# Sixty-four bytes of padding behind one constant: every tile on the left side of SBUF starts half a 128-byte line later

## The chip, the cores and the metric

The kernel runs on one core of one Trainium2 chip. The metric is device time in microseconds (us), the median of the runs shown; lower is better. The core has a matrix engine (PE, with its weight loads shown apart as PEld), a vector engine (DVE), a scalar engine (ACT), a general engine (POOL), a sequencer that mostly issues transfers (SP), and 16 DMA engines. On-chip memory (SBUF) has 128 partitions. A tile takes the same range of bytes in each partition, and "the byte a tile starts at" below is its offset inside a partition. Matrix products accumulate in a separate memory, PSUM.

## The reference

One layer of a streaming encoder on `x` (1, 512, 1024), all in float32:

```python
proj = x @ w_in                       # 1024 x 5704: queries, keys, values of two mixers, index, gates
y_a  = dsa_sequence(q_a, k_a, v_a, q_i, k_i, w_i, rel_bias)   # sparse attention: top-128 keys by an indexer, T5 bias
y_s  = sb_sequence(q_s, k_s, v_s)     # stick-breaking attention, strictly causal
merged = sigmoid(g_a + b0) * (y_a @ w_branch_dsa) + sigmoid(g_b + b1) * (y_s @ w_branch_sb)
x = layer_norm(2**0.25 * x + merged @ w_out)
u, g = split(x @ w_ffn_in)            # 1024 x 5632
h = gelu(causal_dwconv(u)) * g        # width 3, over 2816 channels
x = layer_norm(2**0.25 * x + h @ w_ffn_out)                   # 2816 x 1024
```

The constant of this case is `bgt`, the two gate biases `b0` and `b1`: 16 float32 numbers for each of 128 partitions.

## The kernel before, in words

Every float32 product is made of three matrix multiplications in the type float32r: each operand is split into a high part (ACT copies it to float32r) and a low part (DVE subtracts the high part), and high x high, high x low and low x high are added up in PSUM. A helper, `Stream`, brings the weights: SP issues 512 KB loads into three `raw` buffers, ACT makes `whi` (line 104) and DVE makes `wlo` (line 113), each in three ring buffers. The order of the pieces is one list, and the work of the two mixers is laid out by hand with projections as fillers between the attention heads, so that the matrix engine always has something to do. The scheduler is given ties (`issue_after`) where the order matters.

The stages are: indexer queries and first values (to about 25 us), index scores and key selection, eight stick-breaking heads, eight sparse heads (to about 320 us), the branch products, the output projection (`out_proj`, lines 866 to 868) with the first layer norm, the up-projection of the channel mixing (`ffn_in`, lines 937 to 939, from about 390 us), in which the first down-projection products (`product`, lines 1017 to 1019) are woven in, then the rest of the down-projection in a seven-product scheme, and the second layer norm (to the end at 744.9 us).

In a matrix multiplication one operand is held in the array (stationary, loaded by a PEld instruction) and the other streams through it (moving). In the projections (`proj_t`, lines 233 to 235) and in `ffn_in` the stationary operand is a weight from the ring and the moving one is the activation; in `proj_v` (lines 270 to 272), `out_proj` and `product` the weight is the moving operand.

SBUF is given out as two stacks. The left stack grows up from byte 0 and begins with 16,384 reserved bytes and four small constants; then come the pool `cst` (`ident`, `mhalf`, `bgt`, `cwt`, `wi`), the three `raw` buffers, the ring, and the pools of each stage. The right stack grows down from the top and begins with a pool `edge` that holds one tile of 32 bytes, `rb`; then come the activations `xh` and `xl`, the gate and branch tiles, and later `x1h`, `x1l`, the residual rows `r` and the layer norm's rows. Each allocation is rounded up to 32 bytes. A helper `padded` gives a small tile a whole number of 128-byte units, and nearly all small tiles are made with it:

```python
    def padded(pool, shape, dt=F32, **kw):

        n = int(np.prod(shape[1:]))
        t = pool.tile([shape[0], -(-n // 32) * 32], dt, **kw)[:, :n]
        return t if len(shape) == 2 else t.rearrange("p (a b) -> p a b", a=shape[1])
```

`mhalf` (4 bytes, rounded to 32), `bgt` (64) and `cwt` (352) are not. In the built program `ident` starts at byte 16,512, `mhalf` at 17,024, `bgt` at 17,056, `cwt` at 17,120, `wi` at 17,472, the first `raw` buffer at 17,600. From `wi` on, every tile of the left side starts at byte 64 modulo 128, and so does every tile of the right side (`rb` at 229,312, `x1h` at 170,688).

Of the kernel before, what the change touches and what calls it, by code (L numbers as in the profile page):

```python
# [11 lines left out]
F32 = mybir.dt.float32  # L12
# [115 lines left out]
def tile_block(ctx: ExitStack, tc: tile.TileContext, xT, xN, w_qi, w_ki, w_t, w_v, w_br, w_o, w_fi, w_fo,  # L128
# [10 lines left out]
# [6 lines that stand above are left out]
    cst = ctx.enter_context(tc.tile_pool(name="cst", bufs=1))  # L145
# [74 lines left out]
    nc.gpsimd.memset(mhalf, -0.5)  # L220
    nc.scalar.activation(mhalf, mhalf, AF.Sigmoid)
    nc.gpsimd.memset(mhalf, -0.5)
    bgt = cst.tile([128, 16], F32, name="bgt")
    cwt = cst.tile([128, FC, 4], F32, name="cwt")


# [1072 lines left out]
```

## Time and profile before

| | us |
|---|---|
| median of 3 runs (range) | 747.27 (746.85 to 747.35) |
| span of the profiled execution, first to last instruction | 744.9 |
| median less that span | 2.4 |
| PE busy in that span | 735.6 (99%) |
| PEld, DVE, ACT, POOL busy | 616.9, 572.0, 408.0, 148.8 |

The page shows one execution. PE is busy nearly all the time, the others are not; PEld runs beside PE. The durations of matrix multiplications on the page overlap, so their rate is read from the starts of instructions that follow each other.

### The profile page before, as it was taken

What the parts mean: (1) busy time and instruction counts of PE and PEld (TensorE: products, weight loads), DVE (VectorE), ACT (ScalarE), POOL (GpSimd) and SP (SyncE); (2) the same over time, 40 slices, a digit from 0 to 9 for tenths busy, and PEclk for the clock granted to TensorE, in tenths of its full rate; (3) what the DMA queues carried; (4) which work ended last, traced back from release to release, by engine and by line L of the source; (5) the groups of instructions that cost most, each with busy time, mean ns of one, the idle gap of its engine ahead of it and who ended that gap; (6) DMA issues with size and microseconds to landing.
All of it is one profiled execution on the core that took longest, in us unless ns stands there. A gap on an engine that the chain in (4) does not pass through costs nothing.

```text
span 744.9 us, 9755 instructions
## 1 busy us (share of the span) xinstructions
PE 735.6 (99%) x3477; PEld 616.9 (83%) x3477; DVE 572.0 (77%) x907; ACT 408.0 (55%) x572; POOL 148.8 (20%) x161
## 2 busy tenths in 40 slices
PE   9999999999999999999999999999999999999995
PEld 7888888888888888888889888888888888888885
DVE  5569888999679898668755866686767668668985
ACT  6466867797785587845473533443444344345430
POOL 0002224365743332000101111011101101110011
PEclk9999999999999999999999999999999999999999
DMA  7445887796476455527832544444443444448632
GB/s 266 157 128 188 207 172 173 158 214 163 116 181 154 135 126 136 131 85 247 289 57 86 170 141 142 141 143 143 141 166 114 161 136 149 144 140 268 202 130 84
DMA packets 73631, 117.03 MB, mean 157 GB/s; under 512 B 42536, under 2 KB 42792, under 8 KB 73584
## 3 DMA queue, kind: packets, MB, share of 16 engines
q1 hardware_dynamic: 66304, 93.98, 42.0%
q0 software_dynamic: 5744, 18.38, 9.9%
q10 hardware_dynamic: 1536, 4.06, 2.1%
q8 instruction: 27, 0.44, 0.3%
q14 instruction: 20, 0.16, 0.1%
HBM read 95.93 MB, written 9.98 MB: 142 GB/s over the span
## 4 chain that ended last, share of the span: by engine, by line
PE 89%; DVE 3%; POOL 2%; issue 2%; DMA 2%; ACT 2%; DVEq 0%; POOLq 0%; ACTq 0%
PE u_ps L937 5%; PE u_ps L939 5%; PE g_ps L937 5%; PE u_ps L938 5%; PE g_ps L939 5%; PE g_ps L938 5%; PE m L1019 2%; PE m L1017 2%; PE m L1018 2%; PE av_ps L511 2%; PE ga_ps L234 2%; PE ga_ps L233 2%; PE gb_ps L235 2%; PE gb_ps L234 2%; PE ga_ps L235 2%; PE gb_ps L233 2%
## 5 line engine op out<-in xcount | busy, mean ns | idle before, releaser
L104 ACT ACTIVATE whi<-raw 128x1024 fp32r<-128x1024 f32 (+1 forms) x124 | 123.8, 1001 | 143.1 <-PE g_ps L938 43.7
L113 DVE TENSOR_TENSOR wlo<-raw,whi 128x1024 fp32r<-128x1024 f32 (+1 forms) x105 | 123.9, 1181 | 36.3 <-ACT whi L104 35.6
L939 PE MATMUL u_ps<-x1h,wlo 128*128 128x512 f32 (+1 forms) x192 | 71.4, 372 | 0.0
L937 PE MATMUL u_ps<-x1h,whi 128*128 128x512 f32 (+1 forms) x192 | 71.3, 372 | 0.0
L938 PE MATMUL u_ps<-x1l,whi 128*128 128x512 f32 (+1 forms) x192 | 71.3, 371 | 0.0
L937 PE MATMUL g_ps<-x1h,whi 128*128 128x512 f32 (+1 forms) x184 | 69.9, 380 | 0.0
L938 PE MATMUL g_ps<-x1l,whi 128*128 128x512 f32 (+1 forms) x184 | 69.9, 380 | 0.0
L939 PE MATMUL g_ps<-x1h,wlo 128*128 128x512 f32 (+1 forms) x184 | 69.9, 380 | 0.0
L939 PEld LDWEIGHTS u_ps<-x1h,wlo 128*128 128x128 f32 x192 | 36.2, 188 | 6.3
L938 PEld LDWEIGHTS u_ps<-x1l,whi 128*128 128x128 f32 x192 | 36.2, 188 | 6.3
L937 PEld LDWEIGHTS u_ps<-x1h,whi 128*128 128x128 f32 x192 | 36.2, 188 | 6.2
L939 PEld LDWEIGHTS g_ps<-x1h,wlo 128*128 128x128 f32 x184 | 34.6, 188 | 6.6
L938 PEld LDWEIGHTS g_ps<-x1l,whi 128*128 128x128 f32 x184 | 34.6, 188 | 6.5
L937 PEld LDWEIGHTS g_ps<-x1h,whi 128*128 128x128 f32 x184 | 34.6, 188 | 6.5
L960 DVE TENSOR_TENSOR t<-raw 128x512 f32<-128x512 f32 x11 | 7.6, 693 | 40.1 <-DMA raw<-in_w_fo_dram 39.2
L569 POOL TENSOR_TENSOR bm<-win,score 128x256 f32<-128x256 f32 (+2 forms) x24 | 26.9, 1147 | 32.2 <-DMA pl<-bm 27.3
L985 ACT ACTIVATE c<-c,cwt 128x512 f32<-128x512 f32 x22 | 15.9, 725 | 27.5 <-DVE c L984 27.3
L979 POOL MEMSET u<- 128x2 f32 x22 | 2.1, 98 | 143.7 <-ACT whi L104 99.2
L993 DVE TENSOR_TENSOR hF<-g_ps,c 128x512 f32<-128x512 f32 x22 | 15.1, 687 | 19.7 <-PE g_ps L939 19.7
L835 POOL TENSOR_TENSOR rstd<-rstd,mhalf 128x1 f32<-128x1 f32 x8 | 7.7, 959 | 104.6 <-DVE rstd L834 104.6
L423 DVE MAX8 m<-score 128x8 f32<-128x256 f32 (+2 forms) x48 | 26.6, 556 | 0.9
L557 POOL TENSOR_TENSOR beta<-beta,keep 128x1280 f32<-128x1280 f32 x8 | 21.6, 2704 | 26.7 <-DVE keep L554 26.7
(576 smaller groups left out, 2088.3 us busy)
## 6 DMA issues: line engine op xcount, KB each, us to landing
raw<-in_w_fi_dram SPq DMA_DIRECT2D x44, 512.0 KB, 3.3
raw<-in_w_t_dram SPq DMA_DIRECT2D x32, 512.0 KB, 3.7
raw<-in_w_fo_dram SPq DMA_DIRECT2D x26, 512.0 KB, 4.2
wlo<-in_w_t_dram POOLq DMA_DIRECT2D x14, 512.0 KB, 5.8
raw<-in_w_br_dram SPq DMA_DIRECT2D x8, 512.0 KB, 4.0
raw<-in_w_o_dram SPq DMA_DIRECT2D x8, 512.0 KB, 4.1
raw<-in_w_v_dram SPq DMA_DIRECT2D x7, 512.0 KB, 4.6
raw_b<-in_w_fo_dram SPq DMA_DIRECT2D x6, 512.0 KB, 5.5
```

Of the source, the lines that this page charges most:

```text
L104: self.high = nc.scalar.activation(hi[:, :w], t[:, :w], AF.Copy).ins
L113: self.done[key] = eng.tensor_sub(lo[:, :w], t[:, :w], r32(hi[:, :w])).ins
L233: nc.tensor.matmul(ps[:M], wh[:, c], xh[k], start=(k == 0), stop=False)
L234: nc.tensor.matmul(ps[:M], wh[:, c], xl[k], start=False, stop=False)
L235: nc.tensor.matmul(ps[:M], wl[:, c], xh[k], start=False, stop=(k == KC - 1))
L423: nc.vector.max(m8, sc)
L557: nc.gpsimd.tensor_mul(beta, beta, keep[:, 1:ATT + 1])
L569: nc.gpsimd.tensor_add(bm[:, OFF[j]:OFF[j] + N], win[:, 512 - N:512], score[j])
L937: nc.tensor.matmul(ps[:, c], wh[:, kc], x1h[:, k, c], start=(k == 0), stop=False)
L938: nc.tensor.matmul(ps[:, c], wh[:, kc], x1l[:, k, c], start=False, stop=False)
L939: nc.tensor.matmul(ps[:, c], wl[:, kc], x1h[:, k, c], start=False, stop=(k == KC - 1))
L985: nc.scalar.activation(c, c, AF.Gelu_apprx_tanh, bias=cwt[:, f, 3:4])
```

## The change

`bgt` is made by `padded`: 128 bytes are set aside for it instead of 64, and its 16 numbers stay at the front.

```diff
@@ -220,7 +220,7 @@
     nc.gpsimd.memset(mhalf, -0.5)
     nc.scalar.activation(mhalf, mhalf, AF.Sigmoid)
     nc.gpsimd.memset(mhalf, -0.5)
-    bgt = cst.tile([128, 16], F32, name="bgt")
+    bgt = padded(cst, [128, 16], name="bgt")
     cwt = cst.tile([128, FC, 4], F32, name="cwt")
```

In the two built programs 986 tiles lie in SBUF. 873 of them, all on the left side behind `bgt`, start 64 bytes later: `cwt` at 17,184, `wi` at 17,536 and the first `raw` buffer at 17,664. They start at byte 0 modulo 128 now (`cwt` at 32 instead of 96). The other 113, among them all tiles of the right side, stay where they were. The instructions of each engine, their order, and the semaphores that each waits for are the same in both programs.

## The prediction

> **What bounds the kernel now.** I read the page's first two lines, then the busy time by stage, then the starts of single matrix multiplications.
>
> ```profile
> span 744.9 us, 9755 instructions
> PE 735.6 (99%) x3477; PEld 616.9 (83%) x3477; DVE 572.0 (77%) x907; ACT 408.0 (55%) x572; POOL 148.8 (20%) x161
> 0.00:325.00 325.00, 323.19 (x1556) 271.25 (x1557) 262.69 (x484) 228.43 (x360) 100.57 (x90) 1.00 0.64 162
> 325.00:737.00 412.00, 412.00 (x1922) 345.49 (x1921) 304.82 (x415) 179.54 (x213) 47.27 (x70) 1.00 0.47 154
> 737.00:745.00 8.00, 0.38 (x4) 0.17 (x2) 4.46 (x11) 0.00 (x0) 0.92 (x1) 0.76 0.36 131
> ```
>
> The last three lines are stretches of the span (stretch, length, then busy time and count of PE, PEld, DVE, ACT, POOL, the granted clock, DMA share, GB/s). PE is idle for 1.8 us in the two mixers (325 less 323.19), for nothing at all in the 412 us after them, and for 7.6 us in the tail, where the second layer norm's last rows are made and sent. So the time is a count of matrix multiplications times their spacing, plus about 9.4 us. What does not change that spacing can win at most the 1.8 us, or something of the tail.
>
> The spacing is read from rows of the time line (start, length, engine, line, operation):
>
> ```profile
> 499.63 0.39 PE L1017 MATMUL R<-whi,ah 128*128 128x512 f32 x1
> 499.86 0.39 PE L1018 MATMUL R<-wlo,ah 128*128 128x512 f32 x1
> 500.08 0.39 PE L1017 MATMUL R<-whi,ah 128*128 128x512 f32 x1
> 500.31 0.39 PE L1018 MATMUL R<-wlo,ah 128*128 128x512 f32 x1
> ...
> 501.44 0.39 PE L937 MATMUL g_ps<-x1h,whi 128*128 128x512 f32 x1
> 501.67 0.39 PE L938 MATMUL g_ps<-x1l,whi 128*128 128x512 f32 x1
> 501.90 0.39 PE L939 MATMUL g_ps<-x1h,wlo 128*128 128x512 f32 x1
> 502.12 0.39 PE L937 MATMUL g_ps<-x1h,whi 128*128 128x512 f32 x1
> 399.94 0.28 PE L937 MATMUL u_ps<-x1h,whi 128*128 128x256 f32 x1
> 400.06 0.28 PE L938 MATMUL u_ps<-x1l,whi 128*128 128x256 f32 x1
> 400.18 0.28 PE L939 MATMUL u_ps<-x1h,wlo 128*128 128x256 f32 x1
> 400.30 0.28 PE L937 MATMUL u_ps<-x1h,whi 128*128 128x256 f32 x1
> ```
>
> Three steps of 512 columns take 0.68 us, 226.7 ns each; three of 256 take 0.36 us, 120 ns each. A column therefore costs (226.7 - 120) / 256 = 0.417 ns, and each multiplication carries 226.7 - 512 x 0.417 = 13.3 ns beside its columns. The spacing is the same where both operands come from the left side (line 1017: ring weights stream through `ah`) and where the moving one comes from the right (line 937: `x1h`). Today all of these begin at byte 64 modulo 128, so no row compares residues directly.
>
> **The change part by part.** The change removes no instruction, adds none and moves none; in the built programs order and waits are equal, and no tile of one stage comes to lie on another one that it would newly have to wait for. What it does is 873 new start bytes. I cost them by who reads or writes them.
>
> *Matrix multiplications.* The built program has 3,417 in float32r. In 2,298 the moving operand is on the right and the stationary on the left; in 877 both are on the left; in 242 the moving one is on the left, the stationary on the right. So 1,119 moving operands go from 64 to 0, and 3,175 stationary ones. For the moving side the bound below zero is that the whole 13.3 ns is the price of starting in the middle of a 128-byte line: 1,119 x 13.3 ns = 14.9 us. Two kinds of rows speak to it:
>
> ```profile
> 25.46 0.33 PE L313 MATMUL qi_ps<-xl,whi 128*128 128x384 f32 x1
> 25.64 0.33 PE L312 MATMUL qi_ps<-xh,whi 128*128 128x384 f32 x1
> 271.58 0.34 PE L511 MATMUL av_ps<-ptl,va 128*128 128x384 f32 x1
> 271.75 0.22 PE L511 MATMUL av_ps<-pth,va 128*128 128x128 f32 x1
> ```
>
> Line 313 streams 384 columns in one piece and takes 0.18 us to the next start; line 511 streams three pieces of 128 columns, 1,536 bytes apart, and each piece begins at byte 64 modulo 128. It takes 0.17 us. If a start at byte 64 cost 13.3 ns, two more of them would show as 27 ns. They do not, so I take zero for the moving side and keep the 14.9 us for the range.
>
> The Trainium skill, "TensorE: Matmul & The Clock Gate", section "Back-to-back issue gap", gives N / 2.4 + 2.5 ns, 215.8 ns for 512 columns; the rows above have 226.7, and the rule says nothing of start bytes or of float32r. If the missing 10.9 ns were the start byte, the left-moving 1,119 would give back 12.2 us, and the kernel would take 735.1.
>
> For the stationary side the cover is the multiplication that runs meanwhile:
>
> ```profile
> L939 PEld LDWEIGHTS u_ps<-x1h,wlo 128*128 128x128 f32 x192 | 36.2, 188 | 6.3
> L1018 PEld LDWEIGHTS R<-wlo,ah 128*128 128x128 f32 x22 | 4.1, 188 | 0.9
> ```
>
> A load takes 188 ns inside a spacing of 226.7; a start byte would have to cost 38 ns a load before PE waited at 512 columns. Without that cover, each further ns would cost 3.2 us over 3,175 loads. I take zero.
>
> *DVE, ACT and POOL.* They are late nowhere after 325 us, where PE has no idle time, and their cost there is zero even if they slow a little. Whether they do:
>
> ```profile
> L983 DVE SCALAR_TENSOR_TENSOR c<-u,cwt,c x22: 743/750/1401, 406.8 to 670.1; 128x512 f32<-128x512 f32 x22
> L840 DVE SCALAR_TENSOR_TENSOR r<-r,rstd,ln x14: 745/748/752, 365.6 to 736.5; 128x512 f32<-128x512 f32 x14
> ```
>
> Line 983 (the convolution's middle tap) reads `u` from 4 bytes behind its start, and `c` from its own; line 840 reads two tiles that start alike. The medians are 750 and 748 ns. Two inputs that lie 4 bytes apart in their lines cost 2 ns, so I take zero for 64 bytes as well. The tail's vector instructions read and write `r`, the layer norm's rows and `parts2`, all on the right: unchanged.
>
> *Transfers.* Loads into `raw` began at byte 192 modulo 256 and begin at 0 now; `xr` and `raw_qi`, which the first products wait for, went from 64 to 128.
>
> ```profile
> raw<-in_w_fi_dram SPq DMA_DIRECT2D x44, 512.0 KB, 3.3
> raw<-in_w_v_dram SPq DMA_DIRECT2D x7, 512.0 KB, 4.6
> 0.74 2.79 DMA xr<-in_xT_dram
> ```
>
> Equal loads land 3.3 to 4.6 us after issue depending on what runs beside them, a spread of 1.3 us that PE does not feel after 325 us. Before that, the 1.8 us of idle time bounds any gain. I take -0.1 us, between zero and -1.8, near zero because the ring holds three pieces ahead.
>
> The Trainium skill, "DMA: Bandwidth & Descriptors", section "How a descriptor splits into AXI transactions", says that a descriptor not starting at a multiple of 256 bytes pays for the bytes below its start. By its counting, stated for reads, 4,096 bytes from 192 would take 134 beats and from 0 take 128, 4.5% less. An estimate from it is 0.15 us of a 3.3 us load, and hidden; it speaks for the change, and no row here shows it.
>
> **The sum.** The profiled execution: 744.9 + 0 (moving) + 0 (stationary) + 0 (DVE, ACT, POOL) - 0.1 (transfers) = 744.8. The median of the runs lies 2.4 us above that span (747.27 - 744.9), which the change does not touch: 747.2 us. What a measurement can tell from no change is about 0.2%, 1.5 us: 745.8 to 748.8 counts as the same.
>
> **The rivals.**
>
> *The start byte is part of the 13.3 ns* (faster). For it: the 13.3 ns are there and nothing in the trace explains them, and they are the same for all operands, as they would be if all pay alike. Against it: the three-piece row. In full it gives 747.3 - 14.9 = 732.4; half of it, 739.8. Only left-moving lines (270 to 272, 511, 866 to 868, 1017 to 1019) would speed up, lines 937 to 939 not.
>
> *The two read streams of PE want the same residue* (slower). PE reads the moving operand and the next stationary one at the same time. Today both start at byte 64; afterwards 2,298 + 242 = 2,540 multiplications have one on each side, with residues that differ. For it: PE does run slower in places with no wait shown:
>
> ```profile
> 8.15 0.40 PE L271 MATMUL vs_ps<-wlo,xh 128*128 128x512 f32 x1
> 8.39 0.39 PE L272 MATMUL vs_ps<-whi,xl 128*128 128x512 f32 x1
> ...
> 9.54 0.39 PE L271 MATMUL vs_ps<-wlo,xh 128*128 128x512 f32 x1
> 9.77 0.39 PE L272 MATMUL vs_ps<-whi,xl 128*128 128x512 f32 x1
> ```
>
> Seven steps in 1.62 us are 231.4 ns, 4.7 ns above the steady spacing. At that price 2,540 of them cost 11.9 us: 759.2. It decides from 0.6 ns each (1.5 us). Against it: these slow steps appear with equal residues, and loads and streams are not in step with each other, so a fixed distance between starts need not matter.
>
> *Aligned loads land sooner* (faster, or the same). At most the 1.8 us of idle time before 325 us: 745.5, and for most of its chance under what can be told.
>
> *An engine with tiles on both sides slows* (slower, or the same). 29 two-input DVE instructions and 35 ACT ones touch both sides, few of them in the tail; behind PE they cost nothing, and if each lost 50 ns with PE waiting, 64 x 50 ns = 3.2 us: 750.5.
>
> That the change does not do what it says is excluded by the start bytes of the built program.
>
> **How the numbers follow.** No effect 0.60; start byte in the 13.3 ns 0.14; unequal residues 0.17; sooner loads 0.05, of which 0.03 over 0.2%; two-sided engines 0.04. Faster is 0.14 + 0.03 = 0.17, slower 0.17 + 0.04 = 0.21, the same 0.62. The likeliest case's own range is 745.8 to 748.8. For 8 in 10 I take in the first third of the first rival, down to 742.5 (14.9 / 3 is 5.0 us), and the first half of the second, up to 753.5 (11.9 / 2 is 6.0 us); beyond these I leave 0.09 and 0.08.
>
> **What would show it.** If I am right, the stretch from 325 to 737 us still has PE busy throughout, lines 937 and 1017 step by 226.7 ns, and line 113 keeps its duration. A step of 213 to 220 ns on line 1017 but 226.7 on line 937 is the first rival. A longer step on line 937 alone, or PEld above 188 ns, is the second. Equal steps with a shorter idle time before 325 us is the third; a longer DVE or ACT duration is the fourth.

## The result: 757.75 us, 1.4% slower

| | before | after |
|---|---|---|
| median of the runs compared (range), us | 747.19 (746.85 to 747.35) | 757.75 (757.58 to 758.17) |
| ratio after / before (95% interval) | | 1.0139 (1.0125 to 1.0153) |
| span of the profiled execution, us | 744.9 | 756.0 |

The forecast was 747.2 us, the range 742.5 to 753.5. The change costs 10.6 us in the medians and 11.1 us in the spans. Of all runs in this document one, of the kernel left_plus_256 below, took 1,619 us, for a reason that no trace shows; its median does not hang on it.

The page of after (first two lines), then the busy time by stage with the columns of the prediction's first fence:

```profile
span 756.0 us, 9755 instructions
PE 747.2 (99%) x3477; PEld 616.8 (82%) x3477; DVE 571.3 (76%) x907; ACT 409.4 (54%) x572; POOL 149.3 (20%) x161
```

```profile
0.00:325.00 325.00, 323.81 (x1541) 269.40 (x1542) 261.24 (x482) 228.69 (x359) 101.02 (x90) 1.00 0.63 162
325.00:748.00 423.00, 423.00 (x1936) 347.17 (x1935) 305.42 (x415) 180.71 (x213) 47.34 (x70) 1.00 0.44 150
```

PE is still busy without a gap from 325 us to the tail, at the full granted clock (1.00), and it is busy 11.6 us longer (747.2 against 735.6) for the same 3,477 instructions. DVE, ACT, POOL and PEld are busy as long as before, within 1.4 us each. So no new wait has appeared: the spacing of the matrix multiplications has grown (the idle time of PE before 325 us even fell, from 1.8 to 1.2 us). Where, the first and last starts of two lines tell. The view of one line's instructions (count, shortest, median and longest duration in ns, first and last start in us), of before and then of after:

```profile
L866 PE MATMUL o_ps<-wo0h,mh x8: 389/389/389, 347.3 to 385.4; 128*128 128x512 f32 x8
L939 PE MATMUL u_ps<-x1h,wlo x192: 278/389/389, 391.0 to 667.1; 128*128 128x512 f32 x160, 128*128 128x256 f32 x32
L939 PE MATMUL g_ps<-x1h,wlo x184: 283/389/389, 393.9 to 673.9; 128*128 128x512 f32 x168, 128*128 128x256 f32 x16
```

```profile
L866 PE MATMUL o_ps<-wo0h,mh x8: 388/389/389, 351.5 to 389.6; 128*128 128x512 f32 x8
L939 PE MATMUL u_ps<-x1h,wlo x192: 281/394/398, 395.3 to 677.6; 128*128 128x512 f32 x160, 128*128 128x256 f32 x32
L939 PE MATMUL g_ps<-x1h,wlo x184: 281/394/398, 398.1 to 684.6; 128*128 128x512 f32 x168, 128*128 128x256 f32 x16
```

| stage (from, to) | before, us | after, us | difference |
|---|---|---|---|
| mixers (0 to the first start of line 866) | 347.3 | 351.5 | +4.2 |
| output projection (to the first start of line 939) | 43.7 | 43.8 | +0.1 |
| up-projection (to the last start of line 939) | 282.9 | 289.3 | +6.4 |
| rest of the down-projection, tail (to the span's end) | 71.0 | 71.4 | +0.4 |

The stages that grew are those in which most products have the moving operand on the right side and the stationary one on the left. In the other two both operands come from the left nearly throughout: they moved by the same 64 bytes, and these stages hardly changed. Rows of the time line of after show the two kinds:

```profile
501.01 0.39 PE L938 MATMUL u_ps<-x1l,whi 128*128 128x512 f32 x1
501.25 0.39 PE L939 MATMUL u_ps<-x1h,wlo 128*128 128x512 f32 x1
501.48 0.39 PE L937 MATMUL u_ps<-x1h,whi 128*128 128x512 f32 x1
501.48 0.19 PEld L938 LDWEIGHTS u_ps<-x1l,whi 128*128 128x128 f32 x1
501.71 0.39 PE L938 MATMUL u_ps<-x1l,whi 128*128 128x512 f32 x1
...
361.47 0.39 PE L868 MATMUL o_ps<-wo0h,ml 128*128 128x512 f32 x1
361.70 0.39 PE L866 MATMUL o_ps<-wo1h,mh 128*128 128x512 f32 x1
361.93 0.39 PE L867 MATMUL o_ps<-wo1l,mh 128*128 128x512 f32 x1
362.15 0.39 PE L868 MATMUL o_ps<-wo1h,ml 128*128 128x512 f32 x1
```

Three steps of lines 937 to 939 take 0.70 us, 233.3 ns each (226.7 before); three steps of line 866 to 868 take 0.68 us, 226.7 ns as before. Over the whole trace the mean from the start of a 512-column multiplication to the start of the next one of this size, where the first has its moving operand on the right and its stationary one on the left, goes from 227.3 to 233.2 ns, over 1,958 such steps before and 1,961 after (steps of 260 ns and more, which hold a pause, are left out). Some 1,960 x 5.9 ns are 11.6 us, as much as PE is busy longer; the span grew by 11.1 us, since PE's idle time in the mixers shrank. In the up-projection the step goes from 226.7 to 233.3 ns, in the mixers from 228.0 to 233.1. The steps with both operands on the left go from 226.9 to 227.6, those with a left moving and a right stationary operand from 228.8 to 229.5 (192 and 193 steps); these two together are about 0.5 us. The 256-column steps of lines 937 to 939 went the other way, from 120 to 118 ns (medians), which gives back some 0.3 us.

The work beside PE is as it was. The view of groups of after by shape (busy us, mean ns, idle time before), and its table of DMA issues:

```profile
L939 PEld LDWEIGHTS u_ps<-x1h,wlo 128*128 128x128 f32 x192 | 36.0, 188 | 7.5
L840 DVE SCALAR_TENSOR_TENSOR r<-r,rstd,ln 128x512 f32<-128x512 f32 x14 | 9.8, 751 | 0.0
```

```profile
raw<-in_w_fi_dram SPq DMA_DIRECT2D x44, 512.0 KB, 3.3
```

A weight load still takes 188 ns, only the idle time between loads has grown (6.3 to 7.5 us); the layer norm's DVE step takes what it took, and the median load of the up-projection's weights lands 3.3 us after issue as before.

### The profile page after: what moved, and what is told of

It reads as the page before. It is cut to its first block, busy times and chain, and to the rows that moved or that the text cites. A ratio compares the mean times of both kernels' runs of the same rounds, so it can differ in the third digit from the quotient of the medians.

```text
span 756.0 us, 9755 instructions
## 1 busy us (share of the span) xinstructions
PE 747.2 (99%) x3477; PEld 616.8 (82%) x3477; DVE 571.3 (76%) x907; ACT 409.4 (54%) x572; POOL 149.3 (20%) x161
## 4 chain that ended last, share of the span: by engine, by line
PE 98%; DVE 1%; issue 0%; DVEq 0%
PE u_ps L937 5%; PE u_ps L939 5%; PE g_ps L937 5%; PE g_ps L939 5%; PE u_ps L938 5%; PE g_ps L938 5%; PE av_ps L511 3%; PE m L1018 2%; PE m L1019 2%; PE m L1017 2%; PE ga_ps L234 2%; PE ga_ps L233 2%; PE gb_ps L234 2%; PE ga_ps L235 2%; PE gb_ps L235 2%; PE gb_ps L233 2%
## 5 line engine op out<-in xcount | busy, mean ns | idle before, releaser
L113 DVE TENSOR_TENSOR wlo<-raw,whi 128x1024 fp32r<-128x1024 f32 (+1 forms) x105 | 122.3, 1166 | 39.4 <-ACT whi L104 38.6
```

The source lines that it names most:

```text
L113: self.done[key] = eng.tensor_sub(lo[:, :w], t[:, :w], r32(hi[:, :w])).ins
```

## The experiments

In all of them the instructions, their order and their waits are those of before unless the text says otherwise; only start bytes differ. The operands that count are the weight ring on the left (`whi`, `wlo`) and the activations on the right (`xh`, `xl` in the mixers, `x1h`, `x1l` in the up-projection). Their start bytes in the built programs, modulo 256, with all results of the layer kernels:

| kernel | ring / `xh` / `x1h` | median us | ratio to before (95%) |
|---|---|---|---|
| before | 192 / 192 / 192 | 747.0, 746.9, 747.1 (three comparisons) | |
| after | 0 / 192 / 192 | 757.75 | 1.0139 (1.0125 to 1.0153) |
| both_at_0 | 0 / 128 / 128 | 757.99 | 1.0146 (1.0131 to 1.0161) |
| right_at_0 | 192 / 128 / 128 | 757.59 | 1.0141 (1.0124 to 1.0158) |
| ffn_back | 0 / 192 / 128 | 758.14 | 1.0149 (1.0134 to 1.0164) |
| left_at_96 | 224 / 192 / 192 | 758.46 | 1.0152 (1.0137 to 1.0168) |
| both_follow | 0 / 0 / 0 | 746.63 | 0.9996 (0.9986 to 1.0005) |
| left_plus_128 | 64 / 192 / 192 | 758.15 | 1.0148 (1.0133 to 1.0163) |
| left_plus_256 | 192 / 192 / 192 | 747.07 | 0.9999 (0.9989 to 1.0009) |
| ffn_follow | 0 / 192 / 0 | 751.85 | 1.0069 (1.0054 to 1.0084) |
| bp_plus_128 | 192 / 192 / 192 | 746.53 | 0.9994 (0.9982 to 1.0007) |

### Which start byte is it: equal residues modulo 128, or the left side's own?

Two theories stood after this result. A: the spacing is short where the moving and the stationary operand start alike modulo 128. B: the left side at byte 0 of a line is slow by itself. Four kernels move the one side, the other, or both.

**both_at_0**, the change with the right side moved down by 64 bytes, so that both begin at byte 0 modulo 128:

```diff
 # the kernel after
-    rb = edge.tile([64, H], F32R, name="rb")
+    rb = edge.tile([64, 24], F32R, name="rb")[:, :H]
```

> The changed kernel, with the right side also moved by 64 bytes (the tile rb takes 96 bytes), so that both sides start at byte 0 modulo 128. If unequal starts of the moving and the stationary operand cost time (theory A): the spacing of lines 937 to 939 is back at 226.7 ns and the time at 747.2 us (746.5 to 748.5). If it is byte 0 of the left side itself, whatever the other operand does (theory B): 757.8 us or more, with 233 ns on lines 937 to 939.

Measured: 757.99 us, span 756.0. Theory A's 747.2 is missed; B fits.

**right_at_0**, the kernel before with the same edit of `rb` and `bgt` untouched:

> The kernel before, with only the right side moved by 64 bytes: left at byte 64, right at byte 0 modulo 128. Theory A: the starts differ again, so slow: if the cost is the same in both directions 757.8 us; if the direction matters as lines 270 to 272 of the changed kernel suggest (moving at 0, stationary at 64 there, spacing near 230 ns), +3.3 ns on 2,298 multiplications, 754.8 us. Theory B: the left side is where it was, 747.2 us.

Measured: 757.59 us, span 755.9. Here the left side is where it always was, and the kernel is as slow as after the change. B falls: it is not a matter of the left side's own byte.

**ffn_back**, the change with a small tile more in the pool of the up-projection's activations, which of the operands that count moves `x1h` and `x1l` alone, to byte 0 modulo 128:

```diff
 # the kernel after, behind the allocation of x1l
+    shift = qp.tile([128, 16], F32, name="shift")
```

> The changed kernel, with x1h and x1l alone moved down by 64 bytes, to byte 0 modulo 128 (64 unused bytes stand behind them): only the up-projection has equal starts again. Theory A: its 984 multiplications of 512 columns go from 233.3 to 226.7 ns, 6.6 us less, its 144 of 256 columns from 118 to 120 ns, 0.3 us more: 757.8 - 6.3 = 751.5 us (750.5 to 752.5); the mixers stay slow. Theory B, or a cause outside the matrix engine: 757.8 us.

Measured: 758.14 us, span 756.2. The up-projection, with equal residues modulo 128, gained nothing. A falls too, in the form that it had: with a period of 128 bytes.

**left_at_96**, the kernel before with 32 bytes more for `bgt` instead of 64:

```diff
 # the kernel before
-    bgt = cst.tile([128, 16], F32, name="bgt")
+    bgt = cst.tile([128, 24], F32, name="bgt")[:, :16]
```

> The kernel before, with bgt given 96 bytes: left at byte 96, right at byte 64 modulo 128, starts 32 bytes apart. Theory A with a cost that grows with the distance: 3.3 ns on 2,298 multiplications, about 754 us, and 230 ns on line 937. Theory A with a cost for any inequality: 757.8 us. Theory B (byte 0 is bad, others are not): 747.2 us.

Measured: 758.46 us, span 756.5. Half of the shift costs the whole price, so between 32 and 64 bytes the cost does not grow with the distance. After these four runs the kernel before was fast and every other arrangement slow, and neither theory held.

### The pairs of starts by themselves

**start_map** leaves the layer's work out and streams one tile against another, 24 multiplications in float32r for every pair of start bytes in steps of 16:

```python
for m in range(8):
    for s in range(8):
        ps = bank(f"M{LET[m]}S{LET[s]}")
        for i in range(REP):
            nc.tensor.matmul(ps, sta[:, 4 * s:4 * s + 128], mov[:, 4 * m:4 * m + 512],
                             start=(i == 0), stop=(i == REP - 1))
```

> A kernel that leaves all of the layer's work out and only issues float32r multiplications back to back, 24 for each case, with no other engine at work: the moving operand starts at byte 0, 16, ... 112 of a 128-byte line (letters a to h behind M), the stationary one likewise (behind S), 512 columns; then 384, 256 and 128 columns and bfloat16 for bytes 0 and 64; then pairs that alternate between starts (0, 0) and (64, 64), and between (0, 64) and (64, 0). Theory A: 226.7 ns where the two letters are equal, 233 ns for M at byte 64 and S at byte 0, near 230 the other way round, between these for other distances. Theory B: the spacing depends on S alone. If each multiplication's own two operands decide, the first alternating pair takes 226.7 ns; if the stream and the load of the next operand collide, the second pair does. A cause outside the matrix engine: 226.7 ns everywhere.

Rows of its time line, a row for 24 multiplications (start, length, and the pair: `M` and `S` for moving and stationary, `a` for byte 0, `e` for byte 64; `B` in front for bfloat16). The spacing is the start of the next row less the start of this one, divided by 24:

```profile
37.89 5.75 PE L43 MATMUL MaSe<-mov,sta 128*128 128x512 f32 x24
43.48 5.72 PE L43 MATMUL MaSf<-mov,sta 128*128 128x512 f32 x24
...
192.99 5.67 PE L43 MATMUL MeSa<-mov,sta 128*128 128x512 f32 x24
198.50 5.73 PE L43 MATMUL MeSb<-mov,sta 128*128 128x512 f32 x24
...
215.17 5.62 PE L43 MATMUL MeSe<-mov,sta 128*128 128x512 f32 x24
220.63 5.61 PE L43 MATMUL MeSf<-mov,sta 128*128 128x512 f32 x24
...
414.05 5.34 PE L56 MATMUL BMeSe<-movb,stab 128*128 128x512 bf16 x24
419.23 5.34 PE L56 MATMUL BMeSa<-movb,stab 128*128 128x512 bf16 x24
424.41 5.34 PE L56 MATMUL BMaSe<-movb,stab 128*128 128x512 bf16 x24
```

Moving at 0 and stationary at 64: 5.59 us / 24 = 232.9 ns. Moving at 64 and stationary at 0: 5.51 / 24 = 229.6. Both at 64: 5.46 / 24 = 227.5. So the price is there without the layer, and it hangs on the pair: of the sixteen pairs at multiples of 32 bytes the four with equal starts take 226.7 to 227.5 ns, the other twelve 229.6 to 233.8. Starts at odd multiples of 16 bytes follow no such rule: their equal pairs took 231.3 to 232.9 ns, and some unequal ones about 227. Tiles of the layer are rounded to 32 bytes, so these do not occur there. In bfloat16 the starts make no difference: 5.18 / 24 = 215.8 ns for equal and for unequal ones.

The Trainium skill, "TensorE: Matmul & The Clock Gate", section "Back-to-back issue gap", gives N / 2.4 + 2.5 ns for the isolated gap, 215.8 for 512 columns: the bfloat16 rows agree to the tenth, the float32r rows at equal starts lie 11 ns above, and a start byte does not take them there, since no pair at 512 columns came below 226.7.

Two further groups of this run alternate between the pairs (0, 0) and (64, 64), and between (0, 64) and (64, 0). In the first each multiplication's own operands start alike, in the second each stream and the next load do. Both take about 232 ns a step, worked out from the groups' starts and lengths without the first step. So neither a multiplication's own pair nor its stream and the next load decide alone; at multiples of 32 bytes the short spacing was seen only where both were alike.

Single steps in the layer kernels agree, with the start bytes of the built programs beside the starts in the trace. In the kernel before, 24 steps without a pause lie between two products that each have equal starts but stand 128 bytes (modulo 256) from each other, so that the next load is 128 away from the stream that runs: they take 231.8 ns on average. In bp_plus_128 (below), where all these operands start alike, the same 24 steps take 227.2. The other way round, both_at_0 has 20 steps in which a product's own two starts differ by 128 and the next load starts like the stream: 233.1 ns. Its 18 steps in which both are alike and only the next product's own starts differ take 227.8.

### A period of 256 bytes

A map in which both tiles begin at a multiple of 256 bytes and starts go up to 112 cannot tell a period of 128 from one of 256, and ffn_back had spoken against 128. Theory C: starts must be equal modulo 256. Theory D: only the pair at byte 64 of a 128-byte line on both sides is fast. Four kernels were made for it.

**both_follow**, the change with the right side moved down by 192 bytes, which is 64 bytes up modulo 256, as far as the left side had moved:

```diff
 # the kernel after
-    rb = edge.tile([64, H], F32R, name="rb")
+    rb = edge.tile([64, 56], F32R, name="rb")[:, :H]
```

> The changed kernel (left at byte 0 modulo 256 for the ring) with the right side moved down by 192 bytes (rb takes 224), so that both sides have moved by 64 bytes modulo 256 and the ring, xh and x1h all start at byte 0 modulo 256. Theory C (starts of the two operands must be equal modulo 256): 747.2 us, 226.7 ns on lines 937 to 939. Theory D (only byte 64 modulo 128 on both sides is fast): 757.8 us, since both sides are at 0 modulo 128 here as they were in the first run.

Measured: 746.63 us, span 744.0. The first and the fourth of successive starts in its time line:

```profile
500.61 0.39 PE L937 MATMUL g_ps<-x1h,whi 128*128 128x512 f32 x1
...
501.29 0.39 PE L937 MATMUL g_ps<-x1h,whi 128*128 128x512 f32 x1
```

Three steps in 0.68 us: 226.7 ns again, with the left side where the change puts it. C holds, D falls.

**left_plus_128** and **left_plus_256**, the kernel before with 128 and with 256 bytes more for `bgt`:

```diff
 # the kernel before
-    bgt = cst.tile([128, 16], F32, name="bgt")
+    bgt = cst.tile([128, 48], F32, name="bgt")[:, :16]   # left_plus_128
+    bgt = cst.tile([128, 80], F32, name="bgt")[:, :16]   # left_plus_256
```

> The kernel before with 192 bytes for bgt: the left side moves by 128 bytes, both sides stay at byte 64 modulo 128, but ring and x1h differ by 128 modulo 256. Theory C: 757.8 us, 233 ns on average on lines 937 to 939. Theory D: 747.2 us.

> The kernel before with 320 bytes for bgt: the left side moves by 256 bytes. Theory C and theory D: 747.2 us. A period of 512 bytes or more, or a cause that any move of the left side brings: 757 us or so.

Measured: 758.15 us and 747.07 us. With 128 bytes both sides stand at byte 64 of their 128-byte line, as in the kernel before, and the price is paid in full. The page of left_plus_128:

```profile
span 756.3 us, 9755 instructions
PE 747.5 (99%) x3477; PEld 618.2 (82%) x3477; DVE 571.7 (76%) x907; ACT 408.5 (54%) x572; POOL 149.4 (20%) x161
```

PE is busy 11.9 us longer than before, the others as long within 1.3 us; with 256 bytes PE is back at 736.5.

**ffn_follow**, the change with a larger tile at the same place, which moves `x1h` and `x1l` down by 192 bytes, so that the up-projection's pairs are equal modulo 256 and those of the mixers stay unequal:

```diff
 # the kernel after, behind the allocation of x1l
+    shift = qp.tile([128, 48], F32, name="shift")
```

> The changed kernel with x1h and x1l alone moved down by 192 bytes, to byte 0 modulo 256 like the ring. Theory C: the up-projection's 984 multiplications of 512 columns go from 233.3 back to 226.7 ns and the mixers stay slow: 757.8 - 6.3 = 751.5 us (750.5 to 752.5). Theory D: 757.8 us.

Measured: 751.85 us, span 749.4. Its time line, first and fourth of successive starts in a mixer and in the up-projection (its line numbers behind the edit are one higher, so 938 is line 937 of after):

```profile
92.05 0.40 PE L233 MATMUL ks_ps<-xh,whi 128*128 128x512 f32 x1
...
92.75 0.40 PE L233 MATMUL ks_ps<-xh,whi 128*128 128x512 f32 x1
...
500.05 0.39 PE L938 MATMUL u_ps<-x1h,whi 128*128 128x512 f32 x1
...
500.73 0.39 PE L938 MATMUL u_ps<-x1h,whi 128*128 128x512 f32 x1
```

233.3 ns in the mixer, 226.7 in the up-projection, in one execution. The stages split the same way: from the first to the last start of the up-projection 282.9 us as before the change, and the mixers end at 351.3 us as after it (351.5). One tile of 192 bytes gives back 6.6 us of the span, which is the table's +6.4 within 0.2.

### How the price goes with the distance

**distance_map** takes three starts of the moving operand (0, 64, 128) against 22 of the stationary one, up to 2,048 bytes; otherwise it is start_map.

> As the first map, with no work of the layer: 24 float32r multiplications of 512 columns for each case. The moving operand starts at byte 0 (group A), 64 (B) or 128 (C) of its tile, the stationary one at byte 0, 4, 8, 12, 16, 20, 24, 28, 32, 64, 96, 128, 160, 192, 224, 256, 288, 320, 384, 512, 1024, 2048 (second letter a to v). Theory C: 226.7 ns where the two are equal modulo 256, so in group A at a, p, t, u, v (and within the same 32 bytes as the first map had it, b to h), in group B at j and r, in group C at l and s; 229 to 236 ns elsewhere. A period of 512: p in group A is slow. Theory D: j and r of group B alone.

Rows of its time line with the moving operand at byte 0 (`A`); the stationary one starts at byte 128 (`l`), 160 (`m`), 192 (`n`), 224 (`o`), 256 (`p`), 288 (`q`), 384 (`s`), 512 (`t`) and 1,024 (`u`):

```profile
78.29 5.73 PE L43 MATMUL Al<-mov,sta 128*128 128x512 f32 x24
83.86 5.76 PE L43 MATMUL Am<-mov,sta 128*128 128x512 f32 x24
89.46 5.67 PE L43 MATMUL An<-mov,sta 128*128 128x512 f32 x24
94.97 5.76 PE L43 MATMUL Ao<-mov,sta 128*128 128x512 f32 x24
100.56 5.61 PE L43 MATMUL Ap<-mov,sta 128*128 128x512 f32 x24
106.01 5.75 PE L43 MATMUL Aq<-mov,sta 128*128 128x512 f32 x24
...
117.19 5.74 PE L43 MATMUL As<-mov,sta 128*128 128x512 f32 x24
122.77 5.60 PE L43 MATMUL At<-mov,sta 128*128 128x512 f32 x24
128.21 5.60 PE L43 MATMUL Au<-mov,sta 128*128 128x512 f32 x24
```

Read as before: 128 bytes apart 5.57 / 24 = 232.1 ns, 192 apart 229.6, 256 apart 227.1, 384 apart 232.5, 512 apart 226.7. The period is 256 bytes, out to the 2,048 that were tried, and the price is not proportional to the distance: 32 bytes cost as much as 128 (233.3 for 32). It is not symmetric either: the stationary operand 64 bytes behind the moving one costs some 6 ns, 192 behind (which is 64 ahead, modulo 256) some 3 ns, in this run as in start_map's 232.9 and 229.6. That fits the kernel after: its up-projection has the ring at 0 and `x1h` at 192, so the stationary operand is 64 behind, at 233.2 ns; its products with a left moving and a right stationary operand have it 192 behind, at 229.5 ns. With the moving operand at 64 and at 128 the same holds (equal modulo 256: 226.7 to 227.9), but for a few starts that are no multiples of 32 bytes, which took 226.7 to 227.5 ns though unequal.

The Trainium skill, "SBUF — State Buffer", section "Who interferes with whom", gives PE two read ports, one for the moving operand and one for weight loads, and calls them independent. By that the distance between the two starts would change nothing; in bfloat16 the rows agree (215.8 either way), in float32r they do not (226.7 against 232 and more), and the measurement decides. Whether it is the ports that meet, no run here shows.

### Which sizes feel it

**shape_map** takes four pairs of starts (`a`: 0 and 0, `b`: moving 0 and stationary 64, `c`: 64 and 0, `d`: 0 and 128) and changes the stationary columns (`C`), the streamed columns (`W`) or takes plain float32 (`F`). The theories were C1, that the price grows with the length of the weight load, and C2, that a pair of unequal starts costs a fixed time whatever the sizes.

> As the maps, with no work of the layer: 24 float32r multiplications for each case, at four pairs of starts (last letter: a moving 0 and stationary 0; b 0 and 64; c 64 and 0; d 0 and 128 bytes). Group C: 512 streamed columns over stationary operands of 32, 64, 96 and 128 columns (j to m). Group W: 192, 256, 320, 384, 416, 448, 480 streamed columns (n to t) over 128 stationary ones. Group F: 12 multiplications in plain float32, 512 columns. If the load of the next stationary operand collides with the stream (theory C1), the gap between a and b grows with the stationary columns, from about 1.6 ns at 32 to 6.3 ns at 128, and falls with fewer streamed columns because the load's end takes up the difference. If only the two start bytes matter when a multiplication begins (theory C2), the gap is 6.3 ns in all of groups C and W.

Rows of its time line; `Cj` has 32 stationary columns, `Cm` 128:

```profile
17.17 5.72 PE L44 MATMUL Cja<-mov,sta 128*32 128x512 f32 x24
22.73 5.72 PE L44 MATMUL Cjb<-mov,sta 128*32 128x512 f32 x24
28.29 5.73 PE L44 MATMUL Cjc<-mov,sta 128*32 128x512 f32 x24
...
83.67 5.61 PE L44 MATMUL Cma<-mov,sta 128*128 128x512 f32 x24
89.12 5.76 PE L44 MATMUL Cmb<-mov,sta 128*128 128x512 f32 x24
94.72 5.67 PE L44 MATMUL Cmc<-mov,sta 128*128 128x512 f32 x24
...
217.14 10.46 PE L57 MATMUL Fa<-raw 128*128 128x512 f32 x24
227.44 10.46 PE L57 MATMUL Fb<-raw 128*128 128x512 f32 x24
237.74 10.46 PE L57 MATMUL Fc<-raw 128*128 128x512 f32 x24
```

With 128 stationary columns the price is there: 227.1, 233.3 and 229.6 ns. With 32 columns it is gone, but not as either theory has it: 231.7 ns for the equal pair and for `b`, so equal starts are slow as well (64 and 96 columns: 228.3 to 232.9, with no order in it). At 256 streamed columns the equal pair is the slower one by some 2 ns (120.0 against 117.8, worked out like all that follows from the single starts inside a group), at 192 and 320 all pairs agree (111.6 and 146.7), at 384 to 480 they differ by 2 to 4 ns with changing signs. The starts alone do not even fix the spacing at 256 columns: the pair `c` took 117.8 ns here, and the same pair 113.3 in start_map. In plain float32 every pair takes 10.30 / 24 = 429.2 ns. Both theories fall. What the rows show is narrower: 226.7 ns is a rhythm that float32r finds at 512 streamed and 128 stationary columns with equal starts modulo 256, where successive steps are 226 to 227 ns each; an unequal pair alternates (231, 236, 231, 236 in start_map's `MaSe`).

### Can the kernel before be made better by it?

In the kernel before, the mixers' own tiles behind `rbf` on the left (`kih`, `pth` and others) start at byte 64 modulo 256, while the ring and the activations start at 192. **bp_plus_128** moves them by 128 bytes:

```diff
 # the kernel before
-    rbf = padded(bp, [32, H], name="rbf")
+    rbf = bp.tile([32, 64], F32, name="rbf")[:, :H]
```

> The kernel before with 256 bytes instead of 128 for rbf: the mixers' own tiles behind it (queries, keys, values, attention weights) go from byte 64 to byte 192 modulo 256, where the ring, xh and the branch tiles start. Ring and right side stay. Theory C: dot products of line 406 and 407, whose operands differ by 128 now, come down to the steady spacing, and the fillers that follow an attention product no longer run after operands of another start; at most the 1.9 us that spacings above the steady one cost before 325 us come back: 745.3 to 747.0 us. If the spacing in the mixers has another cause: 747.2 us.

Measured: 746.53 us over 12 runs, ratio 0.9994 (0.9982 to 1.0007), span 744.3. In its profiled execution the 512-column steps before 325 us (again without pauses) lie above 226.7 ns by 1.5 us in sum, in that of before by 1.9 us. That is 0.4 us of the 1.9 that were the most, with the sign that was looked for; the 24 steps of the section on pairs (231.8 to 227.2 ns) are 0.1 us of it. The interval of the ratio holds 1: the time itself does not settle it. Neither this kernel nor both_follow beats the kernel before by anything that can be measured.

## Why the prediction was wrong

**What bounds the kernel: right.** PE is busy throughout, the time is a count of multiplications times their spacing, and the change moved the time through the spacing and nothing else.

**The moving side at zero: right as far as it went.** No pair in the maps came below 226.7 ns at 512 columns, so the 13.3 ns beside the columns hold no start byte that could be won there, and the first rival falls: line 866, with both operands on the left, steps as before. (At 256 columns one unequal pair took 113.3 ns in start_map, below the 120, but 117.8 in shape_map.) But the row that carried this step, three pieces of line 511 against one of line 313, could only speak of the moving operand by itself.

**The stationary side at zero: the step that failed.** It ran: the load's 188 ns lie inside a spacing of 226.7, so a start byte would have to cost 38 ns a load before PE waits. The load still takes 188 ns in the profile of after, and PE slowed by 5.9 ns all the same, on some 1,960 steps: 11.6 us. The cover was counted as if a load could only delay PE by being too long. What counts is how its start byte stands to that of the streamed operand, and the term was costed for each side apart, never for the pair.

**DVE, ACT, POOL and transfers at zero: right.** Line 840 takes 751 ns on average (749 before), line 113's median is 1,221 ns (1,222 before), line 983's 750 in both. The median load of the up-projection's weights lands after 3.3 us in both. The -0.1 us for sooner loads can't be told apart here: the mixers' +4.2 us covers it.

**The second rival: right in its place and nearly in its price, with 0.17 of the chance.** It named the two read streams, a longer step on line 937 (or a PEld above 188 ns, which did not come), and 759.2 us; the median is 757.75. Its 4.7 ns were measured at 5.9 for the products with the moving operand on the right and at 0.7 for those with a left moving and a right stationary one, and its 2,540 multiplications take in shorter ones that pay nothing. That these errors nearly cancel is luck, the more so as the 4.7 ns came from steps that are slow for another reason (below). Its residue was modulo 128, and that is wrong: both_at_0, ffn_back and left_plus_128 restore equality modulo 128 and stay slow, and both_follow, equal modulo 256, is fast. For this edit both periods give the same sign, which is why it came so near.

**The argument against it: wrong.** Loads and streams were said not to be in step with each other. The trace of before says that they are. A row of its time line, to be read with the prediction's start of line 937 at 501.44:

```profile
501.45 0.19 PEld L938 LDWEIGHTS g_ps<-x1l,whi 128*128 128x128 f32 x1
```

The next load starts 0.01 us after the stream does; in the profile of after the two starts fall together (501.48 and 501.48). Over all 984 such steps of lines 937 to 939 the load starts 2 to 4 ns after the stream, in both profiles. So the distance between the two start bytes recurs in the same phase each time, and the chance of the rival should have been higher. The other half of the argument, slow steps of 231.4 ns on lines 271 and 272 at equal residues, is a right observation (they are equal modulo 256 too), but it is no argument: these are the first steps of a rhythm that settles. In the trace of before the steps from 7.92, 12.33 and 27.60 us on, each time directly or one step behind products of 384 columns, last 233, 236, 224, 231, 236, 228, 232 or 233, 231, and then 226 to 227 ns. The group `MeSe` of start_map, equal starts behind a group of unequal ones, begins with 236, 228, 233, 231 and then keeps 226 to 227 as well. So equal starts give 226.7 ns only after some steps of their own. That is the likely reason why the mixers, where sizes alternate, stood at 228.0 ns before the change; it was not tried.

**The range: too short at the slow end.** It took in half of the second rival's price, 753.5 us. For this edit there is no half of it: 32, 64 and 128 bytes cost about the same, and all products of 512 by 128 columns with the moving operand on the right and the stationary one on the left have starts 64 bytes apart. Where a rival is all or nothing, the range either reaches its full price or leaves it out.

**What stays open** is the mechanism inside PE. That the starts' distance modulo 256 decides is shown by the layer kernels and by the maps; that stream and next load meet in SBUF is only argued, and the alternating pairs and the short loads of shape_map speak against the simplest form of it. How the rhythm settles, and why 256 columns or a shorter load behave otherwise, is open as well. An arrangement of the layer with the stationary operand of the right-moving products 192 bytes behind, which by distance_map should pay about half, was not run.

## What to carry to other kernels

Where PE sets the time and its products are float32r at 512 by 128 columns, check that the moving and the stationary operand start at the same byte modulo 256 (at a multiple of 32), on both sides of SBUF, after every edit that changes the size of a tile allocated ahead of them; a constant of 64 bytes cost 1.4% here. That an operation is shorter than the one it runs beside is no proof that it costs nothing: read the spacing from start to start, and cost the pair, not each side. Before ruling out a rival by "not in step", look for the two starts in the time line.

## What the runs showed of the hardware that was not expected

- In float32r, 512 streamed by 128 stationary columns, the spacing is 226.7 to 227.9 ns where the start bytes are equal modulo 256 and multiples of 32, and 229 to 234 ns at all other distances of that kind; starts that are no multiples of 32 are irregular, as told above. bfloat16 (215.8 ns) and plain float32 (429.2 ns a record) do not feel the start bytes.
- Equal starts do not give the short spacing at once: behind products of 384 columns the trace of before shows, at three places, eight steps of 224 to 236 ns first.
- The price depends on the direction: the stationary operand 64 bytes behind the moving one takes 232.9 ns, 192 behind 229.6.
- A shorter weight load is not a faster rhythm: with 32 stationary columns 231.7 ns, slower than the 227.1 of 128 columns at equal starts.
- A start of 64 bytes more changed no duration of DVE, ACT or the transfers that could be seen: packets of 4,096 bytes have a median of 159 ns at start 192 modulo 256 and at 0.
